# The key projection of the attention layer as a stage of its own, by seven half-size products

## The chip, the cores and the metric

The kernel runs on one core of a Trainium2 chip. The metric is the device time of one execution in microseconds (us), as the median of several runs. The engines are PE (TensorE, the matrix engine; PEld is its loading of weights), DVE (VectorE), ACT (ScalarE), POOL (GpSimd) and SP, which in this kernel issues nearly all transfers (DMAs).

## The reference

Two layers run over 640 tokens of width 1024: a prompt of 512, and 8 short requests of 16 tokens each. All values are float32.

```python
# layer 0: gMLP
u, v, z = parts of gelu/linear(h @ w_in)       # h = rms_norm(x)
y = u * (spatial mix of layer_norm(v)) * silu(z)
# layer 1: forgetting attention, 16 heads of 128 channels, E = 2048
proj = h @ w_in                                # 1024 x (4 * 2048 + 16)
q, k, v, z, f = split(proj);  logf = log_sigmoid(f + b_f)
s = (q k^T) * scale + c_i - c_j                # c = cumsum(logf), causal
o = softmax(s) @ v                             # the short requests also read a cache of 256 rows
y = o * silu(z)
# both layers
x = x + rms_norm(y @ w_out);  x = x + sigmoid(x @ w_gate) * (p @ w_proj)
```

k, v and logf of layer 1 are outputs too, next to x and the normalised v of layer 0.

## The kernel before

Every float32 product is made from two rounded halves of each operand: `split` takes the high half on ACT and the rest on DVE, and `mm3` multiplies high by high, high by low and low by high, so each product is three matmuls. Hence each weight goes through four steps: a DMA into a raw slot (`fetch`, tile RAW), the high half on ACT, the low half on DVE (tile W, both in `prefetch`), and then PE. The normalised activations h lie in tile A, high and low, for all 640 tokens. `weights(n)` hands out the next n weight units in the fixed list `units` and lets `prefetch` split as many of those that follow as there is room for.

For u and z of layer 0 the product of a pair of 128 channels with h is made by the Strassen-Winograd scheme (`seven_products`): A and W are cut into quarters, and seven products of 128 x 512 by 512 x 320 replace eight. Left operands are sums of weight quarters, which POOL makes (`left_operands`, tile `sf`); right operands are sums of quarters of h, made once by DVE (`right_operands`, tile `tb`); the results are combined by DVE out of PSUM.

Layer 1 works on pairs of heads, p = 0 to 7. A pair's projection has four parts, `project_v`, `project_k`, `project_q` and `project_z`, each a Python generator which yields after each few matmuls. `channel_steps` makes one head of k, q or z: 8 steps (one for each 128 rows of w_in), each of one 384-token and one 256-token product. k goes from PSUM to SBUF, is transposed on DVE in blocks, and leaves in 16 transfers with rows of 128 bytes.

The attention of pair p is written as small pieces with a time number each (`kv_times`, `sample_times`, `prompt_times`, and loads of the cache `load_k`, `load_v`). `interleave(steps, pieces)` walks the projection of pair p + 1 and puts each piece in once the sum of the yields passes its number. `length` is the sum of the projection's yields, and `step` the distance between pieces of one head. A pair's y (attention output times silu(z)) is stored to DRAM (`store_y`), and read back (`load_y`, `y_again`) for the last stage, `tail`, which multiplies by w_out. z of the last pair is projected after the loop, with a few pieces of that pair's attention between.

A scheduler (Tile) sets each engine's final order from that order of the code and from the tiles that instructions share; all transfers named here stand in SP's queue. A transfer that waits, for a slot for instance, holds up those behind it.

`forget_logits`, `log_forget` and `forget_sums` make logf and its cumulative sums next to the projection of pair 0. Their temporaries come from `tmpa`.

## Time and profile before

| | |
|---|---|
| median of 3 runs | 1342.51 us (1342.37 to 1343.16) |
| profiled execution | 1342.78 us |
| its span, first to last instruction | 1341.0 us |
| mean granted PE clock | 0.997 |
| busy: PE, DVE, ACT, POOL | 99%, 57%, 41%, 10% |
| DMA packets, bytes | 299,913, 172.87 MB |

In a row of a timeline stand the start (us from the span's start), the time, the engine, the line of the kernel, the operation, the output tile and the inputs, the shape, and a count; in brackets how long the engine was idle before, and what ended that. Starts follow each other closer than the durations on PE, since matmuls are pipelined. In a row of a group stand the busy us and the mean ns of one, and then the idle time before.

### The profile page before, as it was taken

How to read it: one execution, taken by the hardware profiler on the slowest of the kernel's cores; microseconds unless marked ns; L12 is line 12 of the kernel's file. 1: busy time of each engine (PE TensorE's matmuls, PEld its weight loads, DVE VectorE, ACT ScalarE, POOL GpSimd, SP SyncE). 2: the span in 40 equal slices, each digit the busy share in tenths (PEclk: the TensorE clock that was granted, in tenths of full speed). 3: DMA queues.
4: the chain of work that ended last, by engine and by line, in shares of the span. 5: the costliest groups of instructions: out<-in, count | busy, mean ns of one | idle time of the engine just before them, and what ended most of it. 6: DMA issues, size and time to landing. Idle time of an engine off the chain costs nothing.

```text
span 1341.0 us, 21534 instructions
## 1 busy us (share of the span) xinstructions
PE 1323.5 (99%) x8363; PEld 1194.5 (89%) x8363; DVE 764.1 (57%) x1581; ACT 543.3 (41%) x1025; POOL 135.1 (10%) x144
## 2 busy tenths in 40 slices
PE   9999899999999999999999999999999999999998
PEld 6788799999988878899999999999999998888786
DVE  7733899899944456543545454445545465544642
ACT  4334544545535334533333343333333344435341
POOL 0012444444000000000000000000000000000100
PEclk9999999999999999999999999999999999999999
DMA  7431522323324204588778586777778687343211
GB/s 243 136 95 50 157 84 77 107 82 97 114 94 157 79 16 126 168 149 157 136 154 177 146 160 147 161 154 140 129 161 166 153 214 224 113 140 120 63 64 47
DMA packets 299913, 172.87 MB, mean 129 GB/s; under 512 B 188769, under 2 KB 269201, under 8 KB 299810
## 3 DMA queue, kind: packets, MB, share of 16 engines
q1 hardware_dynamic: 299666, 171.23, 51.5%
q8 instruction: 65, 1.06, 0.3%
q14 instruction: 38, 0.31, 0.1%
q10 hardware_dynamic: 144, 0.26, 0.1%
HBM read 149.86 MB, written 21.59 MB: 128 GB/s over the span
## 4 chain that ended last, share of the span: by engine, by line
PE 93%; DVE 3%; DMA 1%; ACT 1%; issue 1%; POOL 0%; SPq 0%; DVEq 0%
PE pb L237 28%; PE pb L239 27%; PE pb L238 27%; PE pb L943 3%; PE pb L936 1%; PE pb L997 1%; PE pb L1023 1%; PE pb L275 1%; PE pb L550 1%; DVE W L252 1%; PE pb L1020 1%; DMA R<-in_gmlp_ln_g 1%; DMA RAW<-in_gmlp_w_in 0%; ACT R L459 0%; DMA R<-in_gmlp_ln_b 0%
## 5 line engine op out<-in xcount | busy, mean ns | idle before, releaser
L237 PE MATMUL pb<-A,W 128*128 128x384 f32 (+2 forms) x1024 | 331.2, 323 | 1.8 <-ACT R L521 1.0
L239 PE MATMUL pb<-A,W 128*128 128x384 f32 (+2 forms) x1024 | 318.2, 311 | 0.0
L238 PE MATMUL pb<-A,W 128*128 128x384 f32 (+2 forms) x1024 | 317.5, 310 | 0.0
L237 PE MATMUL pb<-W,A 128*128 128x512 f32 (+1 forms) x840 | 297.4, 355 | 2.2 <-ACT R L669 1.4
L239 PE MATMUL pb<-W,A 128*128 128x512 f32 (+1 forms) x840 | 293.5, 351 | 1.9 <-DVE A L252 1.9
L238 PE MATMUL pb<-W,A 128*128 128x512 f32 (+1 forms) x840 | 293.6, 350 | 0.0
L252 DVE TENSOR_TENSOR W<-RAW,W 128x1024 fp32r<-128x1024 f32 (+1 forms) x156 | 194.9, 1250 | 147.2 <-ACT W L251 142.0
L251 ACT ACTIVATE W<-RAW 128x1024 fp32r<-128x1024 f32 (+1 forms) x156 | 161.4, 1035 | 162.6 <-PE pb L238 71.6
L237 PEld LDWEIGHTS pb<-A,W 128*128 128x128 f32 x1024 | 194.1, 190 | 9.9 <-issue 6.8
L238 PEld LDWEIGHTS pb<-A,W 128*128 128x128 f32 x1024 | 194.1, 190 | 0.6
L239 PEld LDWEIGHTS pb<-A,W 128*128 128x128 f32 x1024 | 193.5, 189 | 0.4 <-issue 0.4
L237 PEld LDWEIGHTS pb<-W,A 128*128 128x128 f32 x840 | 159.1, 189 | 26.6 <-issue 3.1
L239 PEld LDWEIGHTS pb<-W,A 128*128 128x128 f32 x840 | 158.9, 189 | 22.9 <-DVE A L252 2.7
L238 PEld LDWEIGHTS pb<-W,A 128*128 128x128 f32 x840 | 159.0, 189 | 20.2 <-issue 0.4
L252 DVE TENSOR_TENSOR A<-R,A 128x640 fp32r<-128x640 f32 (+1 forms) x51 | 41.0, 835 | 74.2 <-ACT A L251 72.0
L975 DVE STREAM_TRANSPOSE r2b_t<-r2b_t 128x256 f32<-128x256 f32 x128 | 46.4, 414 | 33.8 <-PE pb L997 21.7
L251 ACT ACTIVATE A<-R 128x640 fp32r<-128x640 f32 (+1 forms) x51 | 36.7, 749 | 67.7 <-PE pb L238 65.8
L237 PE MATMUL pb<-tb,W 128*128 128x320 f32 x192 | 60.1, 313 | 0.0
L238 PE MATMUL pb<-tb,W 128*128 128x320 f32 x192 | 59.8, 311 | 0.0
L239 PE MATMUL pb<-tb,W 128*128 128x320 f32 x192 | 59.8, 311 | 0.0
L261 POOL TENSOR_TENSOR SML<-SML 128x1 f32<-128x1 f32 x25 | 17.7, 709 | 392.4 <-DVE SML L259 387.8
L938 ACT ACTIVATE R<-pb 128x128 f32<-128x128 f32 (+1 forms) x64 | 27.9, 436 | 65.0 <-PE pb L936 64.7
(235 smaller groups left out, 1866.5 us busy)
## 6 DMA issues: line engine op xcount, KB each, us to landing
RAW<-in_fox_w_in SPq DMA_DIRECT2D x64, 512.0 KB
RAW<-in_gmlp_w_in SPq DMA_DIRECT2D x40, 512.0 KB
r2b_t<-in_cache_fox_v SPq DMA_DIRECT2D x32, 512.0 KB
r2b_t<-in_cache_fox_k SPq DMA_DIRECT2D x128, 128.0 KB
RAW<-in_gmlp_w_out SPq DMA_DIRECT2D x16, 512.0 KB
RAW<-in_ple_w_gate SPq DMA_DIRECT2D x16, 512.0 KB
RAW<-in_fox_w_out SPq DMA_DIRECT2D x16, 512.0 KB
out<-R SPq DMA_DIRECT2D x40, 128.0 KB
```

The lines of the kernel that those rows point to most:

```text
L237: nc.tensor.matmul(out, lh, rh, start=start, stop=False)
L238: nc.tensor.matmul(out, lh, rl, start=False, stop=False)
L239: nc.tensor.matmul(out, ll, rh, start=False, stop=stop)
L251: nc.scalar.activation(out=hi, in_=src, func=AF.Copy)
L252: nc.vector.tensor_tensor(out=lo, in0=src, in1=f(hi), op=ALU.subtract)
L261: nc.gpsimd.tensor_tensor(out=q, in0=t, in1=mhalf, op=ALU.pow)
L275: nc.tensor.transpose(out=b[:, j * P:(j + 1) * P], in_=src[:, (4 * c + j) * P:(4 * c + j + 1) * P], identity=ident)
L550: nc.tensor.matmul(b0[:, t * P:(t + 1) * P], v_at(pnl, t)[:, c0:c0 + P], wm, start=True, stop=True)
L936: nc.tensor.transpose(out=tb[:, j * P:(j + 1) * P], in_=pr[:, j * P:(j + 1) * P], identity=ident)
L938: nc.scalar.activation(out=pt[:, :n], in_=tb[:, :n], func=AF.Copy)
L943: nc.tensor.matmul(O[:, d], v[:, j, hh * P:(hh + 1) * P], pt[:, j * P:(j + 1) * P], start=(j == 0), stop=(j == i))
L975: nc.vector.transpose(out=kt[:, hh, bl, :PAST], in_=kr[:, hh, bl])
```

## The change

k of all eight pairs is made in a stage of its own (`make_k`), after v, q and z of pair 0 and ahead of the loop, by `seven_products`. `right_operands` runs again for layer 1, with a fourth sum, into a tile (`r2k_t`) that takes the place of `r2b_t` until the stage is over; the temporaries of the forget values move into another tile. k is stored to a DRAM scratch `k_sc`, and `k_again` reads it back, a pair at a time, inside the loop. The 16 output transfers per pair move along. The weight units of k are put together in `units`, with a fourth raw slot in that stretch.

`load_k(0, 0)`, which stood at number 30 in the projection of pair 0, comes after the stage. In the loop all passes have v, q and z with `length, step = 43, 4.2`; up to now passes 0 to 5 had 57 and 5.6 with all four parts, and pass 6 had 43 and 4.2 with v, k and q. z of pair 7 is part of pass 6, and the tail follows the loop with all pieces of pair 7.

```diff
-    def right_operands():
+    def right_operands(t3):
...
-        for o, a, b, dst in ((t_a, b12, b11, 0), (t_b, b22, t_a, 1), (b21, b21, t_b, 2), (b12, b22, b12, None)):
+        for o, a, b, dst in ((t_a, b12, b11, 0), (t_b, b22, t_a, 1), (b21, b21, t_b, 2), (b12, b22, b12, t3)):
...
-    pool2, R2 = second("r2b", F32)
+    pool2, TB = second("r2k", F32R)
+    state["sums"] = r1(10240, 2048)
+    right_operands(3)
-    o = 0
+    o = 4608
     def tmpa(n, p=P):
         nonlocal o
-        res = r2(o, n, p)
+        res = r1(o, n, p)
...
-    def project_k(p):
-        ws = weights(2)
+    def make_k(p):
+        kst = r1((7456, 14272)[p % 2], 2 * TOK)
+        seven_products(lambda i, j: kst[:, i * TOK:(i + 1) * TOK][:, HALF[j]], lambda i, j, c: None, right_sum(3), 12288)
         for hh in range(2):
             h = 2 * p + hh
-            a, b = yield from channel_steps(ws, hh, PRJ)
-            kt, kn = k_of(h), kn_of(h)
-            nc.scalar.activation(out=kt[:, :SA], in_=a[:, :SA], func=AF.Copy)
-            nc.scalar.activation(out=kt[:, SA:], in_=b[:, :P], func=AF.Copy)
-            nc.vector.tensor_copy(out=kn, in_=b[:, P:2 * P])
-            tr = r1(o_kt + hh * TOK, TOK)
-            nc.vector.transpose(out=tr[:, :512], in_=kt)
-            nc.vector.transpose(out=tr[:, 512:], in_=kn)
+            kt = kst[:, hh * TOK:(hh + 1) * TOK]
+            dma(k_sc[h], kt)
+            tr = r1(15552 + hh * TOK, TOK)
+            nc.vector.transpose(out=tr[:, :512], in_=kt[:, :512])
+            nc.vector.transpose(out=tr[:, 512:], in_=kt[:, 512:])
...
+    def k_again(p):
+        for h in (2 * p, 2 * p + 1):
+            dma(k_of(h), k_sc[h][:, :512])
+            dma(kn_of(h), k_sc[h][:, 512:])
...
-    PARTS = (project_v, project_k, project_q, project_z)
-    interleave(project(0, PARTS), [(0.0, forget_logits), (6.0, log_forget), (20.0, forget_sums), (30.0, lambda: load_k(0, 0))])
+    PARTS = (project_v, project_q, project_z)
+    interleave(project(0, PARTS), [(0.0, forget_logits), (6.0, log_forget), (20.0, forget_sums)])
+    for p in range(8):
+        make_k(p)
+    pool2.release()
+    pool2, R2 = second("r2b", F32)
+    load_k(0, 0)
+    k_again(0)
+    length, step = 43, 4.2
     for p in range(7):
-        length, step = (57, 5.6) if p < 6 else (43, 4.2)
-        pieces = kv_times(p, 0, 5) + kv_times(p, 1, length / 2) + sample_times(p, 0, 5) + sample_times(p, 1, length / 2)
-        pieces += [(2, lambda p=p: load_k(p, 1)), (length / 2 - 3, lambda p=p: load_k(p + 1, 0))]
+        late = 4 if p == 0 else 0
+        pieces = kv_times(p, 0, 5 + late) + kv_times(p, 1, length / 2 + late) + sample_times(p, 0, 5 + late) + sample_times(p, 1, length / 2 + late)
+        pieces += [(2 + late, lambda p=p: load_k(p, 1)), (length / 2 - 3 + late, lambda p=p: load_k(p + 1, 0)), (length / 2, lambda p=p: k_again(p + 1))]
         for hh in range(2):
-            pieces += prompt_times(2 * p + hh, 2 + 4 * step * hh, step)
-        interleave(project(p + 1, PARTS if p < 6 else PARTS[:3]), pieces)
+            pieces += prompt_times(2 * p + hh, 2 + late + 4 * step * hh, step)
+        interleave(project(p + 1, PARTS), pieces)
         store_y(p)
     load_y(range(7), 0)
-    now = 14.0
-    pieces = [(now + 0.1, lambda: load_y(range(7, 11), 0)), (now + 20, lambda: load_y(range(11, 14), 0)),
-              (now + 30, lambda: load_y(range(7, 11), 1))]
+    load_y(range(7, 11), 0)
+    pieces = [(13, lambda: load_y(range(11, 14), 0)), (44, lambda: load_y(range(7, 11), 1))]
...
-    interleave(project_z(7), [x for x in pieces if x[0] <= now])
```

The order of an engine's instructions shows three places. `mm3`, `split` and `dma` stand some lines further down in the changed kernel: L237 to L239 become L251 to L253, L252 becomes L266, L115 becomes L117.

First DVE at the forget values, where pair 0 is projected (W are halves of weights, R_69 and r2b_t hold, among other things, the temporaries of `log_forget`). Before:

```order
L252 TENSOR_TENSOR W<-RAW,W 128x1024
L766 TENSOR_TENSOR r2b_t<-r2b_t 128x80
L768 SCALAR_TENSOR_TENSOR r2b_t<-r2b_t 128x80
L770 TENSOR_SCALAR r2b_t<-r2b_t 128x80
L772 SCALAR_TENSOR_TENSOR r2b_t<-r2b_t 128x80
L773 RECIPROCAL r2b_t<-r2b_t 128x80
```

And now:

```order
L266 TENSOR_TENSOR W<-RAW,W 128x512
L772 TENSOR_TENSOR R_69<-R_69 128x80
L877 TENSOR_SCALAR R_69<-pb_70 128x8x16
L774 SCALAR_TENSOR_TENSOR R_69<-R_69 128x80
L266 TENSOR_TENSOR W<-R_69,W 128x1024
L776 TENSOR_SCALAR R_69<-R_69 128x80
L266 TENSOR_TENSOR W<-R_69,W 128x1024
L778 SCALAR_TENSOR_TENSOR R_69<-R_69 128x80
L779 RECIPROCAL R_69<-R_69 128x80
```

Two splits of weight sums (W<-R_69) now stand inside the chain of small instructions.

Then PE between the loop and the tail. L943, later L953, is the last product of pair 6's prompt attention. Before, z of pair 7 (A,W) follows it:

```order
L239 MATMUL pb_73<-A,W 128x256
L943 MATMUL pb_77<-R_69 128x128 x4
L237 MATMUL pb_70<-A,W 128x384
L238 MATMUL pb_70<-A,W 128x384
L239 MATMUL pb_70<-A,W 128x384
```

And now the first products of the tail (W,A) follow it:

```order
L253 MATMUL pb_73<-A,W 128x256
L953 MATMUL pb_77<-R_69 128x128 x4
L1007 MATMUL pb_75<-r2b_t,R_69 32x272 x8
L924 MATMUL pb_76<-R_69 128x128
L251 MATMUL pb_70<-W,A 128x512
```

Of the 107 rows that stood between, z's now stand ahead of L953, and the attention pieces of pair 7 inside the tail.

Last SP at the same place, with the reloads of y (y_sc) for the tail. Before:

```order
L115 DMA y_sc<-R_69 128x640
L115 DMA RAW<-in_fox_w_out 128x2x512
L115 DMA R_69<-y_sc 128x640 x2
L115 DMA y_sc<-R_69 128x640
L115 DMA R_69<-y_sc 128x640
```

And now:

```order
L117 DMA y_sc<-R_69 128x640
L117 DMA A<-y_sc 128x640
L117 DMA RAW<-in_fox_w_out 128x2x512
L117 DMA A<-y_sc 128x640 x3
L117 DMA R_69<-y_sc 128x640 x2
L117 DMA y_sc<-R_69 128x640
```

Four reloads into A, where h was, came behind and stand ahead now.

More of the change, by code (lines that the diff above doesn't have):

```diff
@@ L84, in hybrid_trunk @@
     c_sc = dram.tile([H, SEQ], F32, name="c_sc")
+    k_sc = dram.tile([H, P, TOK], F32, name="k_sc")
     cs_sc = dram.tile([P, 272], F32, name="cs_sc")
@@ L299, in channel_steps @@
             w = [z[:, k % 4, hh * P:(hh + 1) * P] for z in ws[k // 4]]
-            for (a, b), o in zip(splits, out):
+            for (a, b), o in zip(SPLITS, out):
                 mm3(o[:, :b - a], w, h_at(k, a, b), k == 0, k == 7)
@@ L378, in hybrid_trunk @@
     SF = pool2.tile([P, 2560], F32, name="sf")
+    state["sums"] = SF[:, :2048]
     def quarter(i, j):
@@ L444, in hybrid_trunk @@
     load_ln(0)
-    fetch(S0 + 4)
+    fetch(20)
     mu, rs, shift = [], [], []
@@ L534, in seven_products @@
                 total(1, 0, u3, o)
-    def eight_products(done):
-        wz = weights(2)
-        for i in range(2):
-            for j, o in enumerate(channel_unit(wz, i, UZ)):
-                done(i, j, o[:, :HT])
     def gate_spatial(g):
@@ L1091, in hybrid_trunk @@
         pieces += prompt_times(14 + hh, 4 + 21 * hh, 5.2)
-    interleave(project_z(7), [x for x in pieces if x[0] <= now])
     ATT = (5, 6)
     o_junk = r2(9200, 512)
-    tail(1, y_again, (0, 1, 2, 3, 4), [(t - now, g) for t, g in pieces if t > now])
+    tail(1, y_again, (0, 1, 2, 3, 4), pieces)
     pool2.release()
```

79 lines of the change are left out of this document (43 added, 36 removed).

## The prediction

> **What bounds the kernel now.** I read the page's first part, the chain that ended last, and then a table by windows for the stages that the change touches. First the page:
>
> ```profile
> span 1341.0 us, 21534 instructions
> PE 1323.5 (99%) x8363; PEld 1194.5 (89%) x8363; DVE 764.1 (57%) x1581; ACT 543.3 (41%) x1025; POOL 135.1 (10%) x144
> ...
> DMA  7431522323324204588778586777778687343211
> GB/s 243 136 95 50 157 84 77 107 82 97 114 94 157 79 16 126 168 149 157 136 154 177 146 160 147 161 154 140 129 161 166 153 214 224 113 140 120 63 64 47
> ...
> PE 93%; DVE 3%; DMA 1%; ACT 1%; issue 1%; POOL 0%; SPq 0%; DVEq 0%
> ```
>
> PE is busy for 99% of the span and carries 93% of the chain: time falls only if PE gets less work, and every wait that the change puts in front of PE is paid in full. The profiled execution took 1342.78 us around this span; the median of the three runs is 0.27 us lower. A difference under 0.2% (2.7 us, so 1339.8 to 1345.2) could not be told from none.
>
> The windows (start and end, length, then busy us and count for PE, PEld, DVE, ACT, POOL, then clock, DMA share, GB/s): two half-product stages of layer 0 in the first row, the first 55 us of layer 1 in the next two, one pair of the attention loop, and last its p=6 pass, the one with the short time table and no z:
>
> ```profile
> 192.00:219.00 27.00, 27.00 (x192) 26.99 (x191) 24.34 (x39) 12.90 (x24) 12.46 (x9) 1.00 0.29 86
> ...
> 546.00:572.00 26.00, 26.00 (x202) 24.23 (x201) 12.85 (x23) 12.53 (x22) 1.51 (x2) 1.00 0.69 181
> 572.00:601.00 29.00, 29.00 (x190) 27.11 (x189) 13.10 (x28) 8.48 (x15) 1.76 (x3) 1.00 0.83 145
> 693.30:767.20 73.90, 73.90 (x573) 70.27 (x576) 36.04 (x110) 27.21 (x61) 1.40 (x6) 1.00 0.73 156
> ...
> 1062.75:1118.90 56.15, 56.15 (x445) 52.47 (x448) 31.30 (x98) 23.33 (x52) 1.90 (x6) 1.00 0.86 204
> ```
>
> PE has no gap in any of them, at full clock. The resources that are not idle are DVE (24.34 of 27 in the half-product stage) and the DMA engines (0.86 in the short loop).
>
> **PE's work.** Starts of matmuls show what one costs in a dense stretch; their durations overlap. A step of the k projection is three 128x384 and three 128x256 matmuls; a half-size product is made of 128x320 ones:
>
> ```profile
> 599.84 0.34 PE L237 MATMUL pb<-A,W 128*128 128x384 f32 x1
> ...
> 606.04 0.34 PE L237 MATMUL pb<-A,W 128*128 128x384 f32 x1
> ```
>
> ```profile
> 201.03 0.31 PE L237 MATMUL pb<-A,W 128*128 128x320 f32 x1
> ...
> 202.79 0.38 PE L550 MATMUL pb<-R 128*128 128x128 f32 x2
> ```
>
> Seven steps lie between the first two rows, 6.20/7 = 0.886 us each; a pair's k has 16 steps, 14.17 us. Twelve 128x320 matmuls lie between the last two, 1.76/12 = 0.1467 us each; seven products have 7 x 4 x 3 = 84, 12.32 us. That is 1.85 us per pair and **-14.8 us** over eight pairs. Nothing hides this: it is PE's own time.
>
> **The k stage itself.** The durations for what stands beside those 12.32 us:
>
> ```profile
> L252 DVE TENSOR_TENSOR W<-RAW,W 128x1024 fp32r<-128x1024 f32 x148 | 189.4, 1281 | 147.2 <-ACT W L251 142.0 <-DMA out<-R 2.9 <-DMA r2b_t<-in_cache_fox_k 0.8
> L252 DVE TENSOR_TENSOR W<-sf,W 128x1024 fp32r<-128x1024 f32 x32 | 39.2, 1226 | 13.9 <-ACT W L251 13.9
> ...
> L513 DVE TENSOR_TENSOR R<-R,pb 128x320 f32<-128x320 f32 x64 | 29.5, 478 | 0.8
> ...
> L852 DVE STREAM_TRANSPOSE R<-R 128x512 f32<-128x512 f32 x16 | 11.2, 698 | 0.0
> ...
> L252 DVE TENSOR_TENSOR W<-RAW,W 128x512 fp32r<-128x512 f32 x8 | 5.4, 680 | 0.0
> ...
> L853 DVE STREAM_TRANSPOSE R<-R 128x128 f32<-128x128 f32 x16 | 4.6, 286 | 0.0
> ```
>
> DVE per pair: weight splits 1.28 + 2 x 1.23 + 0.68 = 4.4, seven evacuations 7 x 0.48 = 3.4, transposes 2 x (0.70 + 0.29) = 2.0, together 9.8 of 12.32 us, or 0.79; layer 0 held PE dense at 24.34/27.00 = 0.90. So DVE is no bound. DMA per pair: two 512 KB weight units, 640 KB of key outputs (eight stores of 64 KB and eight of 16 KB), 640 KB into k_sc: 2.36 MB in 12.32 us, 192 GB/s. The p=6 pass is the nearest row, with the same key outputs and weights and more small cache-key packets: 204 GB/s at share 0.86 without a PE gap. By it the stage needs 0.86 x 192/204 = 0.81. SP issues 20 transfers:
>
> ```profile
> 643.07 7.29 SPq L115 DMA_DIRECT2D out<-R  x8
> ...
> 660.34 7.88 SPq L115 DMA_DIRECT2D out<-R  x8
> ```
>
> ```profile
> L115 SPq DMA_DIRECT2D out<-R x168: 315/446/3410, 556.6 to 1107.2; - x168
> ```
>
> ```profile
> L115 SPq DMA_DIRECT2D RAW<-in_fox_w_in x59: 367/391/2435, 550.7 to 1075.5; - x59
> ```
>
> At the medians (durations min/median/max in ns) 18 x 0.45 + 2 x 0.39 = 8.9 us, under 12.32. At the rate of the two crowded rows the sixteen key stores alone take 15.2 us, and with two k_sc stores and two weights 16.8: then the queue sets the pair, 4.5 us late, 36 us in all. Behind a late store stand the next pair's weights, and its transposes, which reuse the store's source. I take the medians, since the p=6 row says that these bytes pass: **+0.5 us** for edges; bounds 0 and 36.
>
> **The start of layer 1.** The right-hand sums add eight subtractions and additions and four splits to DVE, just as the projections of pair 0 begin:
>
> ```profile
> L392 DVE TENSOR_TENSOR R<-A 128x1280 f32<-128x1280 f32 x4 | 5.9, 1487 | 0.1
> L394 DVE TENSOR_TENSOR R<-R 128x1280 f32<-128x1280 f32 x4 | 5.9, 1487 | 0.0
> ...
> L252 DVE TENSOR_TENSOR tb<-R,tb 128x1280 fp32r<-128x1280 f32 x3 | 4.4, 1477 | 0.0
> ```
>
> 8 x 1.49 + 4 x 1.48 = 17.8 us. DVE had 55 - 12.85 - 13.10 = 29 us free in 546 to 601, but 14.2 us of PE cover leave pair 0 with its k, and the forget values cannot wait: PE's cumulative sums need DVE's short chain, and in the new order two splits of weight sums stand inside it.
>
> ```profile
> 570.71 0.24 DVE L768 SCALAR_TENSOR_TENSOR r2b_t<-r2b_t 128x80 f32<-128x80 f32 x1
> ...
> 574.39 0.29 DVE L786 TENSOR_TENSOR r2b_t<-CST,r2b_t 128x128 f32<-128x128 f32 x1
> ```
>
> The two splits are 2 x 1.23 = **+2.5 us** if POOL has the sums ready and PE has no cover left. Lower bound 0 (projection matmuls fill it), upper 6, when the splits also wait for POOL. POOL's sums cost, by their inputs:
>
> ```profile
> L186 POOL TENSOR_TENSOR sf<-RAW,sf 128x512 f32<-128x512 f32 x16 | 31.5, 1969 | 1.3
> ...
> L186 POOL TENSOR_TENSOR sf<-R,RAW 128x512 f32<-128x512 f32 x8 | 10.4, 1297 | 24.5 <-DVE W L252 24.5
> ```
>
> Four sums per pair are 5.2 to 7.9 us by these two means. The Trainium skill (SBUF — State Buffer, section "Who interferes with whom") says that a VectorE instruction with two SBUF inputs and a GpSimd instruction that reads SBUF share a port, and that one waits for the other. All twelve new DVE instructions are of that kind, so by this rule the sums go at the slow end, the start costs 2.7 us more, and the sum below would be -3.6 instead of -6.3; the spread of 1297 to 1969 ns for one shape agrees with it but doesn't show the cause.
>
> **The start of the loop.** `load_k(0, 0)` now waits until the stage has released its tile; before, pair 0's projections hid it, and DVE, not PE, waited:
>
> ```profile
> DVE r2b_t L975 <- DMA r2b_t<-in_cache_fox_k: 6.3, 2, 4.1
> ```
>
> The pieces of pass 0 are put 4 units later, and projections stand ahead of them on PE. **+0.5 us**; bounds 0 and 4.1, this wait unhidden.
>
> **The loop.** The time of a pair falls from 73.9 to 59.7 us. Its DMA goes from 156 x 73.9 = 11.5 MB to 10.5 (k weights out, the reload for the key stores): 176 GB/s, share 0.82, under the 0.86 of p=6, which ran PE-dense on the same table. **0 us.**
>
> **The tail's start.** z of the last pair, 14.2 us, stood between the last attention product of pair 6 and the tail; it covered the reload of y. Now the reload's wait is followed at once by the tail.
>
> ```profile
> 1116.09 1.05 PE L943 MATMUL pb<-R 128*128 128x128 f32 x8
> ```
>
> ```profile
> 1116.73 0.80 SPq L115 DMA_DIRECT2D R<-y_sc  x2
> ```
>
> ```profile
> 1133.04 0.74 ACT L251 ACTIVATE A<-R 128x640 fp32r<-128x640 f32 x1 [0.48 <-PE pb L239]
> ```
>
> The second row is the reload, released by the attention product of the first. How long a reload takes to land is not shown; a small store took 1.66 us from its issue to the wait that it ended:
>
> ```profile
> 583.22 0.32 SPq L115 DMA_DIRECT2D c_sc<-r2b_t  x1
> ```
>
> ```profile
> 584.88 0.77 DVE L975 STREAM_TRANSPOSE r2b_t<-r2b_t 128x256 f32<-128x256 f32 x2 [1.35 <-DMA c_sc<-r2b_t]
> ```
>
> With 320 KB at the page's highest rate, 243 GB/s, 1.35 us more: 3.0. Issue 0.40, landing 3.0, split 0.74, less the 1.05 us of eight sample products that PE still has (taken as the first row's x8): 3.1. Ahead in the queue now stand four reloads into A and a weight unit; if all were still moving it would be 7.4. They are released one by one while z ends, so I take **+4.3 us**, nearer the lower end.
>
> **The end of the tail's first pass.** One attention product now comes a matmul late, behind a split of 0.74: **+0.7 us**; bounds 0 and 2.
>
> **Sum.** -14.8 + 0.5 + 2.5 + 0.5 + 0 + 4.3 + 0.7 = -6.3: 1342.78 becomes 1336.5, and on the median's footing **1336.2 us**.
>
> **Rivals.** *The stage is bound by its queue (slower).* Mechanism: sixteen key stores in 12.32 us instead of 73.9. For it: the 7.29 and 7.88 us rows; against: the p=6 row. At 16.8 us per pair 1336 + 36 = 1372; it turns the change slower by over 0.2% from 12.32 + 9/8 = 13.4 us per pair. Chance 0.13. The Trainium skill (DMA: Bandwidth & Descriptors, "Specifications") gives 512 B as the least transfer for full rate, and the key stores are of 128 B; this case shows it only as the rows above.
>
> *The waits add up to the gain (within 0.2%).* Start 6, loop start 2, tail 7.4: -14.8 + 0.5 + 6 + 2 + 7.4 + 0.7 = +1.8, 1344. Each has its row, none a reason to go to its end with the others. Chance 0.16, and 0.02 more that they pass 1345.2.
>
> *The waits are hidden.* Only the tail's 3.1 stays: -11.7, 1330.8; with the reload hidden too, 1327.7. DVE's 29 idle us speak for it. Chance 0.17.
>
> **How the numbers follow.** My forecast has 0.52. Faster is it and the third rival, 0.69; within 0.2%, 0.16; slower 0.15. The range from 1328 to 1347 takes in the third and second rivals and leaves out most of the first.
>
> **What would show it.** In the k stage, twelve starts of 128x320 in 1.76 us, PE busy without a gap, and DMA share about 0.8; a PE gap ended by a weight split whose DMA is late would show the first rival. A PE gap of some 2.5 us ahead of the cumulative sums, ended by DVE; one of about 4 us ahead of the first 128x512 matmul of the tail, ended by ACT's split of the reload. Loop passes of 59.7 us with PE at full share. I'm wrong if passes are longer than that, or the tail's gap over 7.4.

## The result and the profile after

The change made the kernel slower: 1392.24 us (median of four runs, 1387.33 to 1393.01) against 1342.44 us for the kernel before, a ratio of 1.0368 with an interval of 1.0348 to 1.0388. The profiled execution took 1387.33 us, 44.6 us more than that of before; it is the fastest of the four, and the differences in this section are taken from it.

The first part of the page of the changed kernel:

```profile
span 1385.5 us, 21655 instructions
...
PE 1330.9 (96%) x8267; PEld 1190.7 (86%) x8267; DVE 835.2 (60%) x1649; ACT 552.5 (40%) x1021; POOL 178.8 (13%) x176
...
PEclk9999999999999999999997999999999999999999
DMA  7421423332433114337769888888888777333211
...
PE 76%; DVE 9%; DMA 7%; SPq 4%; issue 2%; ACT 1%; POOL 1%; DVEq 0%; ACTq 0%; POOLq 0%
```

PE was 99% busy and is 96%; its share of the chain fell from 93% to 76%, and DVE, DMA and SP's queue have the rest. PE has 96 matmuls fewer, and yet is busy for 7.4 us longer. The span's 44.5 us are thus 37.1 us more of idle PE and 7.4 us more of busy PE. With the 14.8 us of work that went, the busy time should have been 1323.5 - 14.8 = 1308.7: some 22.2 us of it is the same work done slower. The clock accounts for most of that. The trace records when PE's clock was halved: 18.4 us of PE's busy time were lost to it, where before it was 3.4 us, so 15.0 us more. (The mean clock, 0.982 of 1385.5 us after 0.997 of 1341.0, makes it 20.9 us, but 5.5 us of the changed kernel's loss fell into time in which PE was idle anyhow.) The other 7 us are not accounted for.

Windows of the changed kernel (columns as in the prediction's table) show both the idle time and the slow clock: the whole k stage, then stretches of 4 us inside it, and two at the start of the loop.

```profile
620.00:722.00 102.00, 88.42 (x564) 86.59 (x564) 60.14 (x99) 26.79 (x34) 27.46 (x22) 0.95 0.74 157
...
700.00:704.00 4.00, 4.00 (x29) 4.00 (x29) 0.49 (x1) 0.00 (x0) 0.00 (x0) 1.00 1.01 217
708.00:712.00 4.00, 1.96 (x7) 1.96 (x8) 2.37 (x5) 1.92 (x3) 0.00 (x0) 0.60 0.71 142
712.00:716.00 4.00, 4.00 (x18) 4.00 (x17) 3.93 (x8) 0.44 (x1) 0.48 (x2) 0.54 0.40 106
716.00:720.00 4.00, 4.00 (x30) 4.00 (x28) 3.90 (x6) 1.06 (x1) 0.00 (x0) 1.00 0.77 168
...
740.00:744.00 4.00, 0.00 (x0) 0.00 (x0) 0.00 (x0) 0.65 (x1) 0.00 (x0) 0.87 0.90 180
...
756.00:760.00 4.00, 4.00 (x16) 3.60 (x15) 1.57 (x7) 1.25 (x5) 0.69 (x1) 0.50 1.07 129
```

The stage has 13.6 us of idle PE and a mean clock of 0.95. After a gap of 4.33 us that ends at 710.04, PE is busy throughout 712 to 716 and yet does 18 matmuls, where 29 or 30 pass in the windows at full clock: the clock granted is 0.54 on average. After the 10 us at the loop's start it is 0.50 up to 760, though work came back at 749.99. The Trainium skill (TensorE: Matmul & The Clock Gate, "What's actually happening") has this rule: after an idle window of about 3.4 us the clock is halved, until PE has been busy for as long again. The rows agree as to the 0.50, but not as to the idle time that it takes: a gap of 2.56 us with one of 0.58 right behind it was enough (at 796.98), and in the kernel before one of 2.05 (at 166.92). In the trace's record of the clock the halved stretches of this part are 3.4 us long or a multiple of it: 3.4 us behind gaps of 3.87 and 3.98 us, 6.8 behind 4.33 and 4.40, and 17.1 around the gap of 10.43, where full clock came back 9.8 us after the work.

What PE waited for (us in all, how often, the longest):

```profile
PE pb L1007 <- DVE r2b_t L985: 10.4, 1, 10.4
PE pb L251 <- DVE R L526: 7.8, 4, 4.0
PE pb L251 <- ACT A L265: 5.1, 2, 4.4
PE pb L251 <- DVE R L541: 4.7, 2, 4.3
PE pb L789 <- DVE R L782: 3.9, 1, 3.9
```

L526 and L541 are evacuations of the stage, L1007 the first product of the loop with the cached keys, L265 the split at the tail's start, L789 the cumulative sums of the forget values. One step further back, what DVE and ACT waited for in the whole run:

```profile
DVE R L858 <- DMA out<-R: 29.9, 7, 6.8
...
ACT W L265 <- DMA RAW<-in_fox_w_in: 49.3, 13, 9.7
```

L858 is the transpose of a pair's k into the tile from which the previous pair's stores still read. On DVE's timeline the first of these transposes in each pair gives the stage's pace (first and last of eight pairs):

```profile
615.55 0.30 DVE L858 STREAM_TRANSPOSE R<-R 128x128 f32<-128x128 f32 x1
...
723.91 0.32 DVE L858 STREAM_TRANSPOSE R<-R 128x128 f32<-128x128 f32 x1 [2.80 <-DMA out<-R]
```

108.36 us for seven pairs are 15.5 us per pair, where PE's work is 12.32. Matmul starts in a dense piece of the stage confirm the latter: twelve matmuls in 1.76 us.

```profile
639.77 0.31 PE L253 MATMUL pb<-A,W 128*128 128x320 f32 x1
...
641.53 0.31 PE L253 MATMUL pb<-A,W 128*128 128x320 f32 x1
```

### The profile page after: what moved, and what is told of

Its sections match the earlier page's. It is cut to its first block, busy times and chain, and to the rows that moved or that the text cites. A ratio compares the mean times of both kernels' runs of the same rounds, so it can differ in the third digit from the quotient of the medians.

```text
span 1385.5 us, 21655 instructions
## 1 busy us (share of the span) xinstructions
PE 1330.9 (96%) x8267; PEld 1190.7 (86%) x8267; DVE 835.2 (60%) x1649; ACT 552.5 (40%) x1021; POOL 178.8 (13%) x176
## 4 chain that ended last, share of the span: by engine, by line
PE 76%; DVE 9%; DMA 7%; SPq 4%; issue 2%; ACT 1%; POOL 1%; DVEq 0%; ACTq 0%; POOLq 0%
PE pb L251 22%; PE pb L252 22%; PE pb L253 22%; SPq L117 4%; PE pb L953 2%; DVE W L266 2%; DMA out<-R 2%; PE pb L1007 2%; PE pb L946 1%; PE pb L1033 1%; PE pb L289 1%; DMA R<-in_gmlp_ln_b 1%; DMA RAW<-in_fox_w_in 1%; DVE R L526 1%; PE pb L557 1%
## 5 line engine op out<-in xcount | busy, mean ns | idle before, releaser
L251 PE MATMUL pb<-W,A 128*128 128x512 f32 (+1 forms) x840 | 300.3, 359 | 7.1 <-ACT A L265 5.1
L252 PE MATMUL pb<-W,A 128*128 128x512 f32 (+1 forms) x840 | 295.8, 353 | 0.0
L253 PE MATMUL pb<-W,A 128*128 128x512 f32 (+1 forms) x840 | 294.3, 352 | 1.4 <-DVE A L266 1.4
L251 PE MATMUL pb<-A,W 128*128 128x384 f32 (+2 forms) x864 | 280.6, 325 | 7.9 <-DVE R L541 4.7
L252 PE MATMUL pb<-A,W 128*128 128x384 f32 (+2 forms) x864 | 270.1, 313 | 0.0
L253 PE MATMUL pb<-A,W 128*128 128x384 f32 (+2 forms) x864 | 270.1, 313 | 0.0
L266 DVE TENSOR_TENSOR W<-RAW,W 128x1024 fp32r<-128x1024 f32 x154 | 192.0, 1249 | 110.6 <-ACT W L265 107.7
L265 ACT ACTIVATE W<-RAW 128x1024 fp32r<-128x1024 f32 x154 | 156.4, 1016 | 189.8 <-PE pb L252 55.4
L251 PEld LDWEIGHTS pb<-W,A 128*128 128x128 f32 x840 | 160.2, 191 | 33.1 <-ACT A L265 5.7
L253 PEld LDWEIGHTS pb<-W,A 128*128 128x128 f32 x840 | 159.5, 190 | 23.5 <-DVE A L266 2.1
L251 PEld LDWEIGHTS pb<-A,W 128*128 128x128 f32 x864 | 165.4, 191 | 16.1 <-issue 6.4
L252 PEld LDWEIGHTS pb<-W,A 128*128 128x128 f32 x840 | 160.3, 191 | 21.4 <-issue 1.7
L252 PEld LDWEIGHTS pb<-A,W 128*128 128x128 f32 x864 | 165.5, 192 | 1.1 <-issue 0.4
L253 PEld LDWEIGHTS pb<-A,W 128*128 128x128 f32 x864 | 164.8, 191 | 1.3 <-issue 1.3
L266 DVE TENSOR_TENSOR A<-R,A 128x640 fp32r<-128x640 f32 (+1 forms) x51 | 41.3, 836 | 76.4 <-ACT A L265 72.1
L265 ACT ACTIVATE A<-R 128x640 fp32r<-128x640 f32 (+1 forms) x51 | 37.0, 747 | 79.4 <-PE pb L252 66.7
L275 POOL TENSOR_TENSOR SML<-SML 128x1 f32<-128x1 f32 x25 | 17.1, 684 | 390.0 <-DVE SML L273 385.3
L265 ACT ACTIVATE W<-R 128x512 fp32r<-128x512 f32 (+1 forms) x58 | 41.6, 744 | 50.4 <-PE pb L252 27.9
L251 PE MATMUL pb<-tb,W 128*128 128x320 f32 x192 | 59.9, 312 | 0.6 <-DVE R L538 0.6
L252 PE MATMUL pb<-tb,W 128*128 128x320 f32 x192 | 59.6, 311 | 0.0
L253 PE MATMUL pb<-tb,W 128*128 128x320 f32 x192 | 59.5, 310 | 0.0
```

The source lines that it names most:

```text
L251: nc.tensor.matmul(out, lh, rh, start=start, stop=False)
L252: nc.tensor.matmul(out, lh, rl, start=False, stop=False)
L253: nc.tensor.matmul(out, ll, rh, start=False, stop=stop)
L265: nc.scalar.activation(out=hi, in_=src, func=AF.Copy)
L266: nc.vector.tensor_tensor(out=lo, in0=src, in1=f(hi), op=ALU.subtract)
L275: nc.gpsimd.tensor_tensor(out=q, in0=t, in1=mhalf, op=ALU.pow)
```

## The experiments

All were run once each, beside the kernel before on the same chip (1342.2 to 1342.8 us; 1340.3 for the last two). Each is an edit of the changed kernel, unless it says otherwise. The four runs of the changed kernel lie 5.7 us apart (1387.33 to 1393.01), so a difference of that size between two single runs shows nothing.

**What holds the stage.** Either the one source tile of the stores, or the queue behind it. The first experiment gives the transposes two tiles in turn.

```diff
-            tr = r1(15552 + hh * TOK, TOK)
+            tr = r1((15552, 4608)[p % 2] + hh * TOK, TOK)
```

> The changed kernel with a second buffer for the transposed key, so that odd pairs write another one. In the changed kernel's trace the first transposes of the eight pairs lie 15.5 us apart (615.55 to 723.91) where PE has 12.32 us of work, and each waits for key stores of the pair before. Theory 'one buffer': that wait is the reuse of the buffer, the queue itself has room. Then the transposes come 12.3 to 12.8 us apart, the PE gaps of the stage (14 us) go and with them most of the slow clock behind them: 1365 to 1372 us. Rival 'queue': 16 key stores, two weights and two k stores take SP or the DMA engines longer than 12.32 us in any case, so weights come late instead: distance 14 us or more, time 1380 or more.

1392.12 us. DVE's waits for the tile are gone, but the weights come as late as they did (49.3 us in all in the changed kernel), and a pair still takes 14.7 us:

```profile
ACT W L265 <- DMA RAW<-in_fox_w_in: 48.4, 10, 10.8
```

So the tile was at most a small part of what holds the stage; the queue is left. Next, the key stores of pairs 0 to 6 are left out.

```diff
-            for qd in range(4):
+            for qd in range(4 if p == 7 else 0):
```

> The changed kernel with the 16 key output transfers of pairs 0 to 6 left out (those outputs are not written); the transposes and everything else stay. Both theories 'one buffer' and 'queue' put the stage's loss on these stores: first transposes 12.3 to 12.5 us apart, no PE gap in the stage above 0.5 us, 1363 to 1370 us. If DVE, POOL or the weights bound the stage, the distance stays above 14 us. The gap of 10.4 us at the start of the loop is not the stage's: by the theory 'late cache keys' it shrinks by 3 us at most (fewer stores ahead of the cache loads in the queue).

1360.93 us, and PE without a gap from 617 to 705 us. A pair takes 12.32 us. So the stores cost some 31 us (by the median of 1392.24; 26 by the profiled run), clock included, and not all of it in the stage: the wait at L1007, at the loop's start, fell too, from 10.4 to 4.8 us, where at most 3 us were expected. 18.1 us above before remain, though the 14.8 are won: 33 us go elsewhere.

**Bytes or number.** Of the sixteen key stores per pair, eight have 64 KB and eight 16 KB. Each kind was left out alone for pairs 0 to 6.

```diff
+                if p == 7:
                     dma(fk_s[...], ...)      # the 16 KB stores; in the other kernel fk_p, the 64 KB ones
```

> The changed kernel without the eight 16 KB key stores (fk_s) of pairs 0 to 6, which are left out of the outputs; the eight 64 KB ones stay: half the issues, a fifth of the bytes gone. The second buffer (1392 us) did not help and the run without any key store (1361 us, stage dense) did, so the loss is the queue's. Theory 'issues': SP's 16 issues per pair (0.6 us each) bind, so half of them gone frees the stage: 1362 to 1370 us. Theory 'bytes': the DMA engines' time per pair (share 0.76 over 15.5 us in the changed kernel, 11.7 us, of 12.32) binds, so a fifth of the 640 KB (0.9 us) helps a part: 1372 to 1385.

> The mirror: the eight 64 KB key stores (fk_p) of pairs 0 to 6 are left out, the eight 16 KB ones stay: half the issues, four fifths of the bytes gone. 'Issues': as the other half, 1362 to 1370 us. 'Bytes': 3.9 us of DMA time less per pair, stage dense, 1361 to 1366 us; so by 'bytes' this run is at least 8 us faster than the other, by 'issues' the two are alike.

1362.70 us without the small ones, 1366.38 without the large ones. The same window of the two kernels, in this order:

```profile
617.00:705.00 88.00, 88.00 (x607) 88.00 (x606) 66.04 (x106) 27.95 (x35) 33.33 (x24) 1.00 0.82 188
```

```profile
617.00:705.00 88.00, 88.00 (x602) 88.00 (x601) 66.63 (x109) 28.87 (x35) 37.36 (x25) 1.00 0.59 144
```

Both are dense. Taking out 128 KB per pair helped as much as taking out 512 KB; and a stage with a DMA share of 0.82, about the 0.81 that the prediction gave it, does run dense once the transfers are fewer. To turn that round, the third kernel leaves out the 64 KB stores and cuts each 16 KB store in two of 8 KB.

```diff
+                for c in (0, 2):
+                    dma(fk_s[...][:, c:c + 2], trv[qd * 32:(qd + 1) * 32, 16 + c:18 + c])
```

> As the run without the prompt key stores (1366 us; those outputs of pairs 0 to 6 left out), but each of the eight 16 KB sample key stores is cut into two of 8 KB: sixteen transfers per pair again, at a fifth of the bytes of the changed kernel. Theory 'count' (the number of transfers that SP can have under way or issue binds, whatever they carry): the stage is late again, 1378 us or more. Theory 'bytes': 1362 to 1369 us.

1386.49 us: 20.1 us slower than without the cut, with the same bytes and the same rows of 128 bytes. Its stage, which has gaps again at a DMA share of 0.58:

```profile
620.00:725.00 105.00, 96.70 (x639) 95.04 (x638) 63.96 (x106) 27.45 (x34) 28.10 (x24) 0.97 0.58 135
```

A pair takes 14.4 us here ((715.88 - 614.89)/7 by the same transposes), against 15.5 in the changed kernel, which moves 16.27 MB in its stretch to this one's 12.59: with the number kept, the bytes give 1.1 of the 3.2 us that a pair is late; with the bytes kept, the number gives the other 2.1. That is one way to divide it: without the 16 KB stores nearly all the bytes stayed, and the whole 3.2 us went.

The transfers that were issued, counted over the seven pairs of these stretches: 147 in both kernels, or 1.36 per us in the changed one and 1.46 in this one. A pace of 12.32 us per pair would take 147/86.2 = 1.70. At the length that SP's issues have in the changed kernel it could not be reached: the 147 take 87.6 us in all, 0.60 us each, so 21 per pair are 12.5 us. In this one they take 0.47 us each, 9.8 us per pair, so something else holds it. The p=6 pass of the kernel before, on which the prediction leant, issued 61 in 56.15 us: 1.09 per us.

**Is it SP alone?** The weights of the stage are issued from ACT's queue (with two tiles as in the first experiment); the 16 KB stores from ACT's; the 16 KB stores from POOL's.

```diff
-            dma(raw_of(state["raw"])..., ap)
+            (nc.scalar if K0 <= state["raw"] < K1 else nc.sync).dma_start(out=raw_of(...)..., in_=ap)
```

> Two buffers for the transposed key, and the k weights issued from ACT's queue in place of SP's: the same bytes and no wait of weights behind key stores in one queue. Theory 'order' (weights stand behind stores in SP's queue and land 4 to 10 us after their issue): the stage becomes dense, 1363 to 1373 us. Theory 'bytes': the DMA engines are as full as before and the pairs still take 14 to 15 us, 1380 to 1395.

```diff
-                dma(fk_s[...], trv[...])
+                nc.scalar.dma_start(out=fk_s[...], in_=trv[...])     # nc.gpsimd in e14
```

> The changed kernel, all outputs written, with the eight sample key stores of a pair issued from ACT's queue and the eight prompt key stores, weights and k stores from SP's. Theory 'issue time' (SP needs about 0.6 us per transfer, 12.4 us per pair): SP has 12 left, 7.5 us, the stage is dense, 1362 to 1372 us. Theory 'transfers under way' (in the order each transfer also waits for the one that stands eight before it, on either queue): no room is won, 1380 us or more. The weights alone on ACT's queue gave 1384.

> The changed kernel with the eight sample key stores of a pair issued from POOL's queue, whose transfers wait for each other on semaphores of their own, in place of ACT's, whose transfers share the eight with SP's. On ACT (1381 us) SP's issue time was halved and 1.43 transfers a microsecond at 5.0 us from issue to landing kept 7.2 of 8 under way. Theory 'eight under way': with half the stores on other semaphores the stage is dense, 1358 to 1370 us. Theory 'landing' (the DMA engines land small packets no faster in the mix): as on ACT, 1378 or more. POOL may also become the bound by its issues and sums; then PE waits for splits of sums.

1383.76, 1381.13 and 1390.36 us; the last is no gain. With the weights on ACT's queue a pair takes 13.9 us. With the 16 KB stores there it takes 13.5 us ((713.49 - 618.83)/7), and the window has PE at 97.24 of 102 us where it was 88.42. With 143 transfers in 94.7 us it is at 1.51 per us, still short of 1.70, so SP's issuing is not the only bound. In the program the transfers of SP and ACT take eight semaphores in turn, and each waits for the one eight before it, so at most eight of these are under way. How long one is under way (KB each, median us from issue to landing, in the variant with ACT's queue):

```profile
k_sc<-R SPq DMA_DIRECT2D x14, 320.0 KB, 8.1
out<-R SPq DMA_DIRECT2D x52, 64.0 KB, 2.9
...
out<-R ACTq DMA_DIRECT2D x56, 16.0 KB, 4.1
```

Counted from the trace's issues and semaphore updates, some 6.9 are under way on average in this variant's stage and all eight in 40% of the time; in the changed kernel it is 5.4 and 12%. The longest gap of PE in this stage is

```profile
702.15 0.53 PE L251 MATMUL pb<-A,W 128*128 128x320 f32 x1 [3.28 <-DVE R L541]
```

Behind it stand weights that were issued at 687.89 and 688.97. From 690.12 to 696.5 eight transfers are under way and neither queue issues; each of the eight, 16 KB stores too, takes 8.2 to 9.7 us. So here both hold: the eight are full, and what is under way lands late. ACT's queue has a price too. ACT issues in order with its own work, and its splits of weights wait behind its stores (this variant, 610 to 730 us):

```profile
ACT W L265 <- DMA out<-R: 16.0, 2, 9.2
```

No run takes the bound of eight away cleanly. With POOL's queue, which has semaphores of its own, POOL's issues wait for the transposes, and its sums wait behind them:

```profile
POOL out L862 <- DVE R L858: 22.9, 8, 5.4
```

```profile
656.77 2.17 POOL L862 DMA_DIRECT2D out<-R  x4 [1.86 <-DVE R L858]
...
662.36 1.28 POOL L200 TENSOR_TENSOR R<-RAW,R 128x512 f32<-128x512 f32 x1
```

The last sum frees the slot of the next weights. They are issued at 663.41, land 10 us later, and PE waits 7.3 us for their split.

How much of the limit is in SP's issuing, in the eight under way and in the landing of rows of 128 bytes stays open.

**Fewer, wider transfers.** Here PE transposes k (ten 128x128 per pair, one pair late, evacuated by ACT), and five stores of 128 KB with rows of 1 KB take the place of sixteen, with the same bytes.

```diff
+    def k_out(p):
+        kst = r1((7456, 14272)[p % 2], 2 * TOK)
+        for t in range(NT):
+            b = bank((4, 5))
+            for hh in range(2):
+                nc.tensor.transpose(out=b[:, hh * P:(hh + 1) * P], in_=kst[:, hh * TOK + t * P:hh * TOK + (t + 1) * P], identity=ident)
+            st = r1(15552 + t * 256, 256)
+            nc.scalar.activation(out=st, in_=b[:, :256], func=AF.Copy)
+            dma(fk_rows(p, t), st.rearrange("p (h d) -> p h d", h=2))
```

> The changed kernel with k turned by PE (ten 128x128 transposes per pair, one pair late) and stored by token, five transfers of 128 KB in rows of 1024 bytes in place of sixteen with rows of 128: all outputs, the same bytes, nine transfers a pair in the stage in place of twenty. PE gets 80 x 0.13 = 10.5 us more (eight 128x128 products took 1.05 us). Theory 'count': no PE gap in the stage, 1361 (the run without stores) + 10.5 less up to 2 = 1367 to 1374 us. If something else than the stores' number makes the stage late, gaps stay and the time is 1390 or more.

1373.60 us, and the stage is dense from 620 to 692 us with all its bytes (three gaps of 0.6 to 1.2 us follow up to its end). The run changes three things at once, the number, the width of the rows and DVE's transposes, so it shows a way out and not which of them counted. Its window:

```profile
620.00:692.00 72.00, 72.00 (x505) 71.92 (x504) 43.95 (x60) 29.10 (x49) 32.09 (x21) 1.00 0.63 176
```

**Can the loop carry the stores?** In the kernel before it does. Cutting its sixteen key stores per pair into thirty-two costs 3.1 us there (0.2%), so it has room:

```diff
+                for z in range(2):
+                    dma(fk_p[...][:, 8 * z:8 * z + 8], ...); dma(fk_s[...][:, 2 * z:2 * z + 2], ...)
```

> The kernel before with each of the 16 key stores of a pair cut in two: 32 transfers of half the size, in all about 68 a pair in 73.9 us, 0.92 a microsecond. Theory 'eight under way': at some 5 us from issue to landing 4.6 of 8 are under way, there is room, and the time stays within 0.5% of 1342.5 us. Theory 'SP issue time' of 0.6 us: 41 of 73.9 us, also hidden. If the time grows by more than 7 us, a store's cost is not its share of a full queue but a delay of what stands behind it.

1345.27 us against 1342.16. But moving transposes and stores of the changed kernel into its loop made it slower twice, at the end of a pass and, with an earlier reload, at its beginning:

```diff
+                   (length - 10, lambda p=p: k_out(p + 1))     # first; second: (12, k_out(p)), k_again at length / 2 - 8
```

> The changed kernel with the transposes and the 16 key output transfers taken out of the stage and put into the loop, from the k that is read back (pair 0 in pass 0, pair p + 1 late in pass p). By 'one buffer' and 'queue' alike the stage becomes dense (12.32 us per pair). The loop passes get 640 KB more each: by the row of the pass p=6 of before (share 0.86 with the same stores) they stay at 59.7 us, in all 1363 to 1370 us. Rival: the queue is now full in the loop (its share is 0.85 to 0.9 already), passes grow by 2 us or more, 1375 or more.

> Key transposes and stores in the loop again, but those of pair p at number 12 of pass p, when its k has long been read back; in the run before (1440 us) DVE stood up to 11.4 us in front of a transpose whose k was still under way. If that wait was the cause, the passes come back to 59.7 to 62 us and the time to 1360 to 1375 us. If the queue cannot carry the stores in the loop, passes stay above 65 us and the time above 1395.

1439.74 and 1437.80 us. In a stretch of 20 us at the end of a pass of the first one:

```profile
DVE R L861 <- DMA R<-k_sc: 11.4, 1, 11.4
```

DVE takes its instructions in order, and the transpose waits there for k's reload, with the attention's DVE work behind it. The second run shows the same wait (12.2 us): there too the transposes stand a few us behind reloads (952.08 behind 949.20, for one), although the code has them further apart. Whether an earlier reload would do was not run.

**The start of layer 1.** The first sums of weights move from POOL to DVE, to see whether POOL's reading slows DVE's short forget chain.

```diff
-                nc.gpsimd.tensor_tensor(out=o, in0=a, in1=b, op=op)
+                (nc.vector if i == K0 else nc.gpsimd).tensor_tensor(out=o, in0=a, in1=b, op=op)
```

> The changed kernel with the four weight sums of the first k pair on DVE in place of POOL. In the changed kernel's trace DVE's 128x80 steps of the forget values take 1.13 to 1.35 us while POOL makes sums, and took 0.24 us before. Theory 'port' (DVE with two inputs in SBUF and POOL keep each other waiting): they come back to 0.24 us, and the cumulative sums start 4 to 6 us earlier although DVE has 2.8 us more to do. Rival 'order': they are late because of what stands ahead of them, and stay over 1 us or as late. The total moves little, 1385 to 1393 us, since the stage's loss remains.

1385.77 us, no clear difference in all. PE's wait ahead of the cumulative sums falls from 3.87 to 0.84 us; but it also varies in runs without this edit, from 1.3 to 4.1 us, and only together with the wait ahead of the forget logits (L760) is it steadier: 4.4 to 6.8 us without the edit, 2.3 here and 4.2 in the last run below, which has the edit too. And the sums don't start 4 to 6 us earlier, as expected, but at 600.74, after 598.80; from L760 on the chain takes 33.1 us and took 33.7. What is clear is the single step of the chain, in the changed kernel and in this one:

```profile
588.91 1.25 DVE L774 SCALAR_TENSOR_TENSOR R<-R 128x80 f32<-128x80 f32 x1
```

```profile
590.05 0.23 DVE L774 SCALAR_TENSOR_TENSOR R<-R 128x80 f32<-128x80 f32 x1
...
599.09 1.32 DVE L781 TENSOR_TENSOR R<-R 128x80 f32<-128x80 f32 x1
```

```profile
599.03 1.28 POOL L200 TENSOR_TENSOR R<-RAW,R 128x512 f32<-128x512 f32 x1
```

The last two rows are of one time: the DVE step that runs beside a remaining POOL sum takes 1.32 us, up to the end of that sum (600.31, to within 0.1). So the rule of the port that the prediction weighed holds for the steps; that the start of layer 1 is much shorter without it is not shown.

**The start of the loop.** First its pieces are put later (14 units, not 4).

```diff
-        late = 4 if p == 0 else 0
+        late = 14 if p == 0 else 0
```

> The changed kernel with late = 14 in place of 4 in pass 0, so that 10 units more of projections stand ahead of the first cache pieces. Theory 'late cache keys': the gap of 10.4 us ahead of the first sample scores is the time from the release of the tile to the landing of the cache keys; 10 us more of PE work cover it, the clock stays up, and the kernel takes 1370 to 1378 us. Rival: pieces that are pushed past the end of pass 0 leave gaps there, and the gain is under 5 us.

1397.75 us: of the gap of 10.4 two of 1.4 and 2.3 are left, and gaps of 1.9, 5.7, 4.7, 2.0 and 2.7 us stand further on, where the pieces crowd into what is left of the pass. Next, on top of the variant with ACT's queue, the first cached keys are read during the stage, into room that is free then, and late is 0.

```diff
-        kr = r2(o_K, 2048).rearrange...
+        kr = (r1(5408, 2048) if i == 0 else r2(o_K, 2048)).rearrange...
...
+        if p == 3:
+            load_k(0, 0)
```

> The run before plus the loop's start: the first cache keys are loaded into another tile during the stage (after pair 3), and late is 0. Theory 'late cache keys': the first gap of the loop (10.4 us in the changed kernel, 4.8 to 7.5 where the stage was dense) falls under 1 us, with the slow clock behind it, 10 to 15 us less than the half-on-ACT run. Rival: the eight loads of 128-byte rows now stand among the stage's transfers and cost there what they save.

1377.20 us, only 4 us better, where 10 to 15 were expected; in the variant that it stands on, the wait at L1007 was 3.6 us already. PE no longer waits for cached keys, but for other steps of the first attention:

```profile
743.07 0.48 PE L946 MATMUL pb<-CST,r2b_t 128*128 128x128 f32 x1 [7.08 <-DVE r2b_t L940]
```

**The start of the tail.** On top of that, the first two reloads of y go to where k was, which is free earlier.

```diff
-            return r1(g * TOK, TOK)
+            return r1(o_kt + g * TOK if g < 2 else g * TOK, TOK)
```

> The same plus the tail's start: y of heads 0 and 1 is read back into a place that is free during the whole loop, so that it doesn't wait for the last attention product of pair 6. Theory 'reload': the gap of 4.4 us ahead of the tail's first product and its slow clock go, 5 to 8 us less than the run before this. Rival: the split of y on ACT and DVE is late for another reason, under 2 us less.

1369.27 us, 7.9 us better; the gap at the tail's start is gone. It had been 5.1 us in the kernel without this edit. The rest is not told apart: it may be clock, but gaps in the stage were shorter in this run too (4.1 us behind L534, after 7.0).

**All together.** The last two edits on the variant with POOL's queue, and then on the wide stores with DVE's first sums:

> Half the stores on POOL's queue, the first cache keys loaded early into another tile, and the free place for y of heads 0 and 1: three of the losses mended together. If each theory holds, the stage loses under 3 us, the loop's start under 3, the tail's start nothing, and what stays is the start of layer 1 (5 us and slow clock): 1335 to 1348 us. The same mending with ACT's queue gave 1369.

> The same with the other three places mended: the first k pair's sums on DVE, the first cache keys loaded into another tile during the stage, y of heads 0 and 1 read back into a free place. If the losses are independent, 3 us come back at the start, 8 to 10 at the loop's start and 8 at the tail (each with its slow clock): 1346 to 1356 us, still above the kernel before, since PE's transposes take 10.5 of the 14.8 us won. If they hide each other, over 1358.

1378.93 us, where 1335 to 1348 were expected: a pair of that stage still takes 14.9 us. 1352.17 us for the second, whose longest waits are these:

```profile
PE pb L251 <- DVE SML L1015: 5.5, 1, 5.5
PE pb L760 <- DVE WF L266: 4.2, 1, 4.2
```

It is the best version of the change, and 0.9% slower than the kernel before: its 80 PE transposes, in the group below (busy time, overlapped with the matmuls around them), take back most of the 14.8 us, and the two gaps above are left, one at the start of layer 1 (566.8 us) and one in the first pass (760.8). No version that was run beats the kernel before.

```profile
L864 PE MATMUL pb<-CST,R 128*128 128x128 f32 x80 | 13.1, 273 | 0.8 <-ACT R L866 0.8
```

## Why the prediction was wrong

By its steps, in the order of its sum (1336.2 forecast, 1392.24 measured; by the profiled execution -6.3 forecast, +44.5 in the span):

- **PE's work, -14.8: right.** 1.76 us for twelve matmuls, as shown. The gain is there; it was spent elsewhere.
- **The k stage, +0.5: this step failed.** It is the first rival, slower by the mechanism that the rival names, at a pace of 15.5 us per pair (the rival's price was 16.8, its threshold 13.4). Over the seven pairs shown that is 22.1 us, where the sum has 0.5 for all eight. I had both rows in hand, the crowded stores and the dense p=6 pass, and took the second as nearer because its bytes pass. But p=6 spreads 61 transfers over 56 us; the stage has to pass 1.70 per us. The estimate by bytes (share 0.81) was not wrong as such: it says nothing on a limit that is in the number. The medians of SP's issues fail with it: they gave 8.9 us per pair, and in the stage the mean of 0.60 us gives 12.5. Idle PE is 13.6 us of it, as the stage's groups show:

```profile
L251 PE MATMUL pb<-r2k_t,W 128*128 128x320 f32 x128 | 41.4, 323 | 7.2 <-DVE R L526 7.2
...
L251 PE MATMUL pb<-A,W 128*128 128x320 f32 x96 | 30.6, 318 | 6.4 <-DVE R L541 4.3 <-ACT R L534 2.0
```

- **The start of layer 1, +2.5: too small, inside its bounds.** 1.27 + 3.87 = 5.1 us. The two splits are in the chain, as forecast; the small steps between them are five times longer (0.24 to 1.3 us) beside POOL's sums. The Trainium skill's sentence (SBUF — State Buffer, "Who interferes with whom"), which the sum left out, would have given 5.2 as the prediction priced it, on POOL's side; the trace has the cost on DVE's too. That it comes so near is luck in part, since 1.27 of the 5.1 us is a wait ahead of the forget logits, which neither figure had.
- **The start of the loop, +0.5: this step failed too.** 10.43 + 2.56 + 0.58 = 13.6 us, far over its upper end of 4.1. That end was the wait for cached keys in a queue that is not full. Here the loads stand in SP's queue behind the last pair's late stores:

```profile
740.66 3.12 SPq L117 DMA_DIRECT2D out<-R  x6
743.88 5.73 SPq L117 DMA_DIRECT2D r2b_t<-in_cache_fox_k  x8
```

```profile
749.99 1.09 PE L1007 MATMUL pb<-r2b_t,R 128*32 128x272 f32 x2 [10.43 <-DVE r2b_t L985]
```

  The projections that I counted on as cover ran out at 739.56, before the loads were issued. The runs that took the cause away found the next waits right behind it: this seam needs the whole first pass to be placed anew.
- **The loop, 0: right.** A pass takes 59.7 us, dense, at a DMA share of 0.75 (0.82 forecast):

```profile
1104.70:1164.40 59.70, 59.70 (x474) 56.06 (x473) 33.88 (x105) 25.55 (x59) 2.24 (x6) 1.00 0.75 185
```

- **The tail's start, +4.3: right**, 4.40 us, by the mechanism named (the reload, then ACT's split). That it fits to 0.1 us is luck: the worked-out end was 3.1, with 3.4 us from issue to landing, which took 5.5, and the upper end of 7.4 doesn't follow from its terms (1.84 MB at 243 GB/s are 7.6 us more, so 10.6).

```profile
1168.76 5.48 DMA R<-y_sc
```

```profile
1175.05 0.80 PE L251 MATMUL pb<-W,A 128*128 128x512 f32 x1 [4.40 <-ACT A L265]
```

- **The end of the tail's first pass, +0.7:** 0.52 + 0.69 = 1.2 us, one of them as before.
- **What the sum did not have: the clock.** Every gap was priced at its own length. Idle PE grew by 37.1 us, and slower work cost 22.2 more, 15.0 of them at the halved clock: 0.4 us for each us of gap, or 0.6 with the part that is not accounted for. Even the tail's 4.4 us, priced rightly, stands in a stretch, from pair 6's last attention product to the end of the span, that is 6.6 us longer (217.38 us, after 224.91 with z's 14.17 in it).

In sum -14.8 + 37.1 + 22.2 = 44.5 (the 22.2 being what the other two leave), where the 37.1 are mostly the stage (13.6), the loop's start (13.6), layer 1's start (5.1) and the tail (4.4). The chance of 0.13 for the first rival was too low: nothing in the profile of before showed sixteen stores passing in 12 us, and the only two rows that showed them close together were slow. The experiments show that the stores hold the stage, more by their number than by their bytes, and that DVE's steps are slow beside POOL's sums. That the late stores push the loop's start is shown by SP's order in the rows above; how much of it is theirs is not. The wait at L1007 is 4.8, 7.5 and 6.7 us in the three runs with fewer stores, but 5.2 also with two tiles and all sixteen.

## What to carry to other kernels

When a change packs the same transfers into a shorter stretch, count transfers per us as well as bytes, and compare with the busiest stretch that the profile shows dense; above that rate an average share of the DMA engines proves nothing. Price a new PE wait of some 2 to 3 us or more with the slow clock behind it, here 0.4 to 0.6 us for each us of wait. And where a stage is cut out of a pipelined loop, look at both seams: each loses the work that covered its loads.

## What the hardware showed that I had not expected

- A limit that goes more by number than by bytes: on SP's queue 1.36 transfers per us with 16.27 MB in the seven pairs' stretch and 1.46 with 12.59 MB, and 1.51 with ACT's queue beside it; the stretches at 1.09 and below were dense. Between 1.09 and 1.36 no run lies, and what sets the limit is open. The Trainium skill (DMA: Bandwidth & Descriptors, "Rules for kernel authors") says that transfers under 64 KB are mostly overhead; leaving out eight of 16 KB or eight of 64 KB did the same for the stage, which goes further than the rule.
- The halved clock after gaps: 0.54 for 4 us behind a gap of 4.3 us, 0.50 for 10 us behind one of 10.4. Gaps of 3.87 and 3.98 did it too, and the one of 2.56 with one of 0.58 behind it. Behind gaps of 1.86 us, at 647.66, and 2.02, at 669.33, it was 1.00; the 2.05 of the kernel before halved it, so near 2 us the length of a gap alone does not decide. First the window behind the 2.56, then that behind the 1.86:

```profile
796.00:800.00 4.00, 3.42 (x13) 3.04 (x14) 3.09 (x13) 2.67 (x7) 0.00 (x0) 0.70 0.70 208
```

```profile
648.00:652.00 4.00, 4.00 (x29) 3.91 (x28) 3.93 (x6) 1.08 (x3) 0.00 (x0) 1.00 0.92 198
```

- DVE steps on 128x80 took 0.24 us alone and 1.1 to 1.35 beside a POOL sum of 128x512, ending with it. A step with a single tile as input did so too (both rows from the run with the first sums on DVE, beside a sum that stayed on POOL):

```profile
592.90 1.14 DVE L776 TENSOR_SCALAR R<-R 128x80 f32<-128x80 f32 x1 [0.35 <-ACT R L775]
```

```profile
592.68 1.30 POOL L200 TENSOR_TENSOR R<-RAW 128x512 f32<-128x512 f32 x1 [34.20 <-DVE W L266]
```
